# First stage of a DiT trunk on one Trainium2 core: 24 instead of 32 modulation halves on TensorE, row norms and gates taken earlier, background pieces begun later

## The chip, the cores and the metric

The kernel runs on one core of a Trainium2 chip. The metric is the device time of one execution in microseconds, as a median of several runs. All times of single instructions below come from one profiled execution of the kernel before.

## The reference

Batch 1, 256 rows of x and 256 rows of ctx, width 2048, two layers, everything in float32. Cut to what matters here:

```
def reference(x, c, ctx, c_ctx, w_ada, ...):
    for layer in range(2):
        # six modulation vectors a layer, for x and for ctx
        mx = split(silu(c) @ w_ada[layer] + b_ada[layer], 6)
        mc = split(silu(c_ctx) @ w_ada[layer] + b_ada[layer], 6)
        h_x = rms_norm(x, g_pre_mix[layer]) * (1 + mx[1]) + mx[0]
        if layer == 0:                       # ctx feeds layer 0 alone
            h_c = rms_norm(ctx, g_pre_mix[0]) * (1 + mc[1]) + mc[0]
            y_x = attention_deltanet_mixer(h_x, h_c, w_in, ...) @ w_out
        else:
            y_x = fourier_mix(h_x) @ w_fourier
        x = x + mx[2] * rms_norm(y_x, g_post_mix[layer])
        f_x = swiglu(rms_norm(x, ...) * (1 + mx[4]) + mx[3], w_gate, w_up, w_down)
        x = x + mx[5] * rms_norm(f_x, g_post_ffn[layer])
    return x

def deltanet_inputs(qkv_raw, a_raw, b_raw, w_conv, a_log, dt_bias):
    ...                                      # conv, silu, l2 norms of q, k, v
    beta = sigmoid(b_raw)
    g = -exp(a_log) * softplus(a_raw + dt_bias)   # the gates
```

The weights are read from HBM once, some 600 MB in all, and each projection is done as three matmuls on a weight that is split into a rounded part `whi` and a rest `wlo`.

## The kernel before

The kernel is one program whose work is put into engine queues at build time; every engine then runs its queue in order. The text below is about its first stage, which ends near 195.5 us, and about the background work that follows it.

**First stage.** The first two modulation vectors of layer 0 (for x and for ctx) come from a matrix `ada_s`, cut into 32 pieces (16 column blocks `k` times two vectors `m`) of two halves each, 64 halves of 512 KB. `ada_half` (L341 on) loads one half (L346) into the next tile of a ring of borrowed buffers (`RING0`, `RING`) and computes it on one of two engines, by the letter that `WHO` has for its piece. A half on TensorE ("p") is 8 float32 matmuls with 2 columns (16 entries in the trace), which serve x and ctx at once; after the second half ScalarE copies the two sums into `aacc` (tile names K, L354). A half on VectorE ("d") is two multiply-and-sum instructions `ada_dot` (L274) over 128x1024, one for x with the row vector `cb`, one for ctx with `KTOK` or `VTOK`. `WHO` is 'pd' sixteen times: half of the pieces on each engine.

**Norms and transposes.** For ctx and then for x, ScalarE sums the squares of both row blocks (L389, with a ZT buffer as scratch), `rstd` (L305 on: a square root on ScalarE, the rest on VectorE) gives the reciprocal norms, VectorE scales the identity with them into `dg` (L392), and TensorE multiplies the rows with `dg`, which transposes and normalises at once (`turned`, 32 matmuls of 128 columns each for ctx and for x, each of them two entries in the trace). `PRE` says how many halves are put in between: four at each of four places.

**Projection.** Then a loop over 16 blocks `k` runs, with halves issued up to index 4k+8, `mod_k(k-1)` (VectorE adds the sums of a block into `gz`, L419 to L421, ScalarE and GpSimd make the modulated input `hT`) and `proj_k(k-2)`: 42 float32r matmuls of 256 columns against one 128x928 block of `w_g0`, whose `whi` is made on ScalarE (L197) and whose `wlo` on VectorE (L203). `w_g0` holds the first heads of the delta-net and the 32 columns of its gates (`pab`).

**Gates.** After the loop the gates are computed: transposes of `pab` on TensorE, then `exp_fine` (L449 on; an exponential and a logarithm on ScalarE and four small instructions on VectorE) on 128 columns, one more logarithm (L480), and `exp_fine` again on 16 columns of the constant vector `smallr`, whose result is `ea`; `gg` (L484) needs both. ScalarE must load another function table each time that it changes between silu, exponential and logarithm.

**Background.** The ten later modulation vectors come from `ada_d`, 320 pieces of 512 KB. Each is a DMA into one of the two `araw` buffers and one `ada_dot` on VectorE (L285, L274). During the mixer one piece is put in whenever the builder's count of TensorE time has moved on by `MRATE` = 4.3 us (`every`, L147; `step`, L581). Later stages put in pieces at rates of their own, and `ada_until` puts in at once what a stage needs and hasn't got (among them, at the Fourier layer's output projection, up to nine vectors).

## Time and profile before

| what | us |
|---|---|
| median of 3 runs | 2524.68 |
| lowest and highest | 2523.31, 2525.12 |
| profiled execution, its own time | 2527.05 |
| span of its trace | 2525.2 |
| TensorE busy in the span | 2388.6 (95%) |
| VectorE busy | 1775.6 (70%) |
| ScalarE busy | 1274.6 (50%) |
| GpSimd busy | 332.5 (13%) |

The mean granted clock of TensorE is 0.97 of full speed. An engine's busy share is an average over the whole span; the first stage is some 8% of it. In the views, PE is TensorE, DVE is VectorE, ACT is ScalarE, POOL is GpSimd and SP is the engine that issues the loads.

### The profile page before, as it was taken

The numbers are of one execution on the slowest core, as the hardware profiler recorded it, in microseconds if no ns is written. First come the engines' busy times: TensorE is split into PE (matmuls) and PEld (weight loads), VectorE is DVE, ScalarE is ACT, GpSimd is POOL, SyncE is SP. The second block draws the span as 40 slices with busy tenths as digits, with TensorE's granted clock in tenths as the row PEclk, the third lists the DMA queues.
The fourth block names the chain that finished last, engine by engine and source line by source line (L and its number), as shares of the span: only waits on it lengthen the run. The fifth ranks groups of instructions, "written<-read, shape, count | busy, mean of one in ns | idle before, by whom it ended". The sixth has DMA issues, their size and how long they took to land.

```text
span 2525.2 us, 39613 instructions
## 1 busy us (share of the span) xinstructions
PE 2388.6 (95%) x14520; PEld 2022.8 (80%) x14520; DVE 1775.6 (70%) x3204; ACT 1274.6 (50%) x2298; POOL 332.5 (13%) x286
## 2 busy tenths in 40 slices
PE   7999888978799999999999999899999999999997
PEld 7998678867677788888888887697788888888886
DVE  4678788778657777877778788747666665555556
ACT  3337433544465654554445454646654554445455
POOL 1214434245431100000000000101100000000001
PEclk7999989989899999999999999999999999999998
DMA  6675778677837569999898998636577777666665
GB/s 252 244 288 197 236 224 272 208 245 253 263 130 237 197 228 316 312 312 317 319 318 312 315 322 308 211 102 217 191 235 242 232 237 234 193 191 189 191 201 191
DMA packets 218483, 611.04 MB, mean 242 GB/s; under 512 B 68905, under 2 KB 69913, under 8 KB 217521
## 3 DMA queue, kind: packets, MB, share of 16 engines
q1 hardware_dynamic: 168016, 581.59, 68.7%
q10 hardware_dynamic: 46528, 15.21, 2.6%
q0 software_dynamic: 3744, 11.71, 1.4%
q8 instruction: 114, 1.87, 0.3%
q14 instruction: 81, 0.66, 0.1%
HBM read 595.03 MB, written 13.40 MB: 241 GB/s over the span
## 4 chain that ended last, share of the span: by engine, by line
PE 70%; DVE 10%; DMA 6%; issue 3%; ACT 2%; POOL 1%; SPq 0%; ACTq 0%; DVEq 0%; POOLq 0%
PE acc L132 65%; PE sm L132 4%; DMA araw<-in_ada_d 4%; DVE araw L274 3%; DVE S L1153 1%; PE sm L1236 1%; DVE wlo L203 1%; POOL wlo L203 1%; ACT whi L197 1%; DVE C L513 1%; DVE T L729 0%; DMA T<-dy 0%; DVE T L731 0%; DMA T<-dz 0%; DMA raw<-in_w_dn 0%
## 5 line engine op out<-in xcount | busy, mean ns | idle before, releaser
L197 ACT ACTIVATE whi<-raw 128x512 fp32r<-128x512 f32 (+1 forms) x1306 | 817.9, 630 | 858.4 <-DVE wlo L203 489.1
L203 DVE TENSOR_TENSOR wlo<-raw,whi 128x512 fp32r<-128x512 f32 x1140 | 788.7, 699 | 469.8 <-ACT whi L197 468.1
L132 PE MATMUL acc<-whi,S 128*128 128x512 f32 x3312 | 1047.1, 394 | 8.1 <-ACT whi L197 3.7
L132 PEld LDWEIGHTS acc<-whi,S 128*128 128x128 f32 x3312 | 626.7, 190 | 139.5 <-ACT whi L197 4.5
L132 PE MATMUL acc<-wlo,S 128*128 128x512 f32 x1656 | 651.0, 393 | 3.8 <-DVE wlo L203 1.9
L274 DVE SCALAR_TENSOR_TENSOR araw<-araw,cb 128x1024 f32<-128x1024 f32 x320 | 415.6, 1300 | 66.9 <-DMA araw<-in_ada_d 66.3
L132 PEld LDWEIGHTS acc<-wlo,S 128*128 128x128 f32 x1656 | 314.1, 190 | 69.0 <-POOL wlo L203 2.9
L203 POOL TENSOR_TENSOR wlo<-raw,whi 128x512 fp32r<-128x512 f32 x166 | 245.7, 1493 | 445.2 <-ACT whi L197 429.3
L132 PE MATMUL acc<-S,whi 128*128 128x256 f32 x1152 | 235.1, 296 | 5.1 <-ACT whi L197 3.4
L132 PEld LDWEIGHTS acc<-S,whi 128*128 128x128 f32 x1152 | 193.3, 201 | 5.8 <-ACT whi L197 3.6
L132 PE MATMUL acc<-S,wlo 128*128 128x256 f32 x576 | 169.7, 296 | 2.0 <-POOL wlo L203 2.0
L1113 POOL DMA_DIRECT2D drow<-K x4 | 2.0, 508 | 1273.9 <-DVE K L1111 1273.9
L132 PE MATMUL acc<-whi,ZT 128*128 128x512 f32 x384 | 122.1, 392 | 0.0
L132 PEld LDWEIGHTS acc<-S,wlo 128*128 128x128 f32 x576 | 115.9, 201 | 3.5 <-POOL wlo L203 2.6
L132 PE MATMUL acc<-whi,KCH 128*128 128x512 f32 x320 | 110.7, 402 | 1.1 <-ACT whi L197 1.1
L132 PE MATMUL acc<-whi,A 128*128 128x512 f32 x312 | 106.0, 395 | 0.0
L132 PE MATMUL acc<-whi,T 128*128 128x512 f32 x296 | 99.5, 392 | 0.0
L132 PEld LDWEIGHTS acc<-whi,ZT 128*128 128x128 f32 x384 | 72.1, 188 | 15.3
L132 PE MATMUL acc<-wlo,KCH 128*128 128x512 f32 x192 | 78.0, 406 | 4.3 <-DVE wlo L203 4.1
L132 PE MATMUL acc<-wlo,ZT 128*128 128x512 f32 x192 | 75.6, 394 | 0.2 <-POOL wlo L203 0.2
L132 PEld LDWEIGHTS acc<-whi,KCH 128*128 128x128 f32 x320 | 62.2, 195 | 15.2 <-ACT whi L197 1.5
L132 PE MATMUL acc<-wlo,T 128*128 128x512 f32 x176 | 68.8, 391 | 0.0
(437 smaller groups left out, 2829.2 us busy)
## 6 DMA issues: line engine op xcount, KB each, us to landing
raw<-in_w_gu SPq DMA_DIRECT2D x347, 512.0 KB, 4.4
araw<-in_ada_d SPq DMA_DIRECT2D x320, 512.0 KB, 4.8
raw<-in_w_dn SPq DMA_DIRECT2D x179, 512.0 KB, 4.4
raw<-in_w_att SPq DMA_DIRECT2D x40, 512.0 KB, 4.4
raw<-in_w_gdn SPq DMA_DIRECT2D x34, 512.0 KB, 4.8
raw<-in_w_out SPq DMA_DIRECT2D x30, 512.0 KB, 3.7
ZT<-in_ada_s SPq DMA_DIRECT2D x24, 512.0 KB, 3.7
raw<-in_w_four SPq DMA_DIRECT2D x21, 512.0 KB, 3.7
```

The lines of the kernel that those rows point to most:

```text
L132: nc.tensor.matmul(out, l, r, start=start, stop=stop)
L197: S.activation(hi[:, :w], raw[:, c:c + w], AF.Copy)
L203: eng.tensor_sub(lo[:, :w], raw[:, c:c + w], hi[:, :w].bitcast(F32))
L274: V.scalar_tensor_tensor(out=junk, in0=w, scalar=1.0, in1=rows, op0=ALU.mult, op1=ALU.mult, accum_out=dst)
L513: V.scalar_tensor_tensor(out=ca[:, :, lo:hi], in0=pv[:, :, lo + o:hi + o], scalar=wconv[:, blk, j:j + 1], in1=ca[:, :, lo:hi], op0=ALU.mul ...
L1113: nc.gpsimd.dma_start(drow.rearrange("h k p -> (h k) p"), gt)
L1153: V.scalar_tensor_tensor(out=x[:, t, sl], in0=y[:, t, sl], scalar=r, in1=x[:, t, sl], op0=ALU.mult, op1=ALU.add)
L1236: nc.tensor.transpose(p[:, i * P:(i + 1) * P], hv[t][:, i * P:(i + 1) * P], ident)
```

## The change

It does six things.

1. `WHO` becomes 'pd' four times and then 'pdd' eight times: 12 pieces on TensorE instead of 16 (24 halves and not 32), 20 on VectorE instead of 16 (40 halves and not 32).
2. `PRE` becomes (2, 6, 4, 4).
3. All four sums of squares are put in first, one `rstd` works on four columns, and four scalings of the identity follow; before, ctx's norms were done ahead of x's squares.
4. `exp_fine` moves up, and `ea` is computed at the very start.
5. In `proj_k` the gates' 32 columns come first and not next to last.
6. After `every(MRATE)` the due time of the first background piece is moved on by `QUIET` = 24 us of counted TensorE time.

```
-WHO = 'pd' * 16
-PRE = (4, 4, 4, 4)
+WHO = 'pd' * 4 + 'pdd' * 8
+PRE = (2, 6, 4, 4)
 LEAD = 8
+QUIET = 24.0
...
+    ea = C([P, 16], "ea")
+    V.tensor_copy(ea, exp_fine(smallr[:, 1, :], [P, 16]))
...
     for i, (src, name) in enumerate(srcs):
         for t in range(2):
             S.activation(zt([P, D], BF16), src[:, t], AF.Square, accum_out=ssq[:, 2 * i + t:2 * i + t + 1])
-        r0 = rstd(ssq[:, 2 * i:2 * i + 2], 2, D)
+    r0 = rstd(ssq, 4, D)
+    for i in range(2):
         for t in range(2):
-            V.tensor_scalar_mul(dg[:, i, t], ident, r0[:, t:t + 1])
+            V.tensor_scalar_mul(dg[:, i, t], ident, r0[:, 2 * i + t:2 * i + t + 1])
+    for i, (src, name) in enumerate(srcs):
         halves(PRE[2 * i])
...
     def proj_k(k):
         w = wk.pop(k)
+        mm3w(pab[0:32], w[1], slice(2 * P, 2 * P + 32), k, k == 0, k == KC - 1)
         for b in range(4):
...
-        mm3w(pab[0:32], w[1], slice(2 * P, 2 * P + 32), k, k == 0, k == KC - 1)
         mm3w(p1, w[1], slice(2 * P + 32, 3 * P + 32), k, k == 0, k == KC - 1)
...
-    ea = exp_fine(smallr[:, 1, :], [P, 16])
...
     every(MRATE)
+    pace[1] += QUIET
```

`exp_fine` itself is the same at its new place, and its lines, like all that stand below a new line, have other numbers in the changed kernel: L274 is L275 there, L457 is L338, L459 is L340, L480 is L486, L516 is L521, L419 to L421 are L441 to L443, L203 is L204.

**VectorE at the very start, before.** `col` holds the norms, `C` is `dg`, the tiles `araw_213` and `KCH_217` are halves:

```order
L308 TENSOR_SCALAR col_180<-col_169 128x2
L310 RECIPROCAL col_179<-col_179 128x2
L312 TENSOR_TENSOR col_184<-col_179 128x2
L313 TENSOR_TENSOR col_184<-col_184,col_180 128x2
L314 TENSOR_SCALAR col_184<-col_184 128x2
L315 TENSOR_TENSOR col_179<-col_179,col_184 128x2
L392 TENSOR_SCALAR C_26_170<-ident,col_179 128x128 x2
L375 COPY T_17_161<-sm_221 128x2x256
L274 SCALAR_TENSOR_TENSOR E_16_160,K_15_157<-araw_213,cb 128x1024
```

The same place in the changed kernel (`K_17_167` is `aacc`):

```order
L309 TENSOR_SCALAR col_194<-col_179 128x4
L275 SCALAR_TENSOR_TENSOR E_18_170,K_17_167<-araw_253,cb 128x1024
L311 RECIPROCAL col_193<-col_193 128x4
L275 SCALAR_TENSOR_TENSOR E_18_170,K_17_167<-araw_253,KTOK_107 128x1024
L313 TENSOR_TENSOR col_198<-col_193 128x4
L275 SCALAR_TENSOR_TENSOR E_18_170,K_17_167<-KCH_257,cb 128x1024
L314 TENSOR_TENSOR col_198<-col_198,col_194 128x4
L275 SCALAR_TENSOR_TENSOR E_18_170,K_17_167<-KCH_257,VTOK_108 128x1024
L315 TENSOR_SCALAR col_198<-col_198 128x4
L441 TENSOR_REDUCE gz<-K_17_167 128x4
L316 TENSOR_TENSOR col_193<-col_193,col_198 128x4
L413 TENSOR_SCALAR C_28_180<-ident,col_193 128x128 x4
```

The norms now stand between the four dots of the first two VectorE halves, and `dg` comes behind those and behind the first block's sum. (Two small instructions on `gz`, L442 and, behind `dg`, L443, aren't shown; the first stands between the last two rows.)

**VectorE in a step of the projection loop, before.** `wlo` of one `w_g0` block in two parts, the dots of two halves, one sum:

```order
L203 TENSOR_TENSOR wlo_1061<-raw_1058,whi_1060 128x512
L274 SCALAR_TENSOR_TENSOR E_16_160,K_15_157<-araw_1002,VTOK_108 128x1024
L203 TENSOR_TENSOR wlo_1065<-raw_1058,whi_1064 128x416
L419 TENSOR_REDUCE gz<-K_15_157 128x4
L420 TENSOR_TENSOR gz<-gz,bada 128x4
L421 TENSOR_SCALAR gz<-gz,gains 128x2
L274 SCALAR_TENSOR_TENSOR E_16_160,K_15_157<-ZT_1090,cb 128x1024
L274 SCALAR_TENSOR_TENSOR E_16_160,K_15_157<-ZT_1090,KTOK_107 128x1024
L274 SCALAR_TENSOR_TENSOR E_16_160,K_15_157<-ZT_1094,cb 128x1024
```

A step at about the same place in the changed kernel, from one `wlo` to the next:

```order
L204 TENSOR_TENSOR wlo_1033<-raw_1030,whi_1032 128x512
L275 SCALAR_TENSOR_TENSOR E_18_170,K_17_167<-araw_974,cb 128x1024
L204 TENSOR_TENSOR wlo_1037<-raw_1030,whi_1036 128x416
L275 SCALAR_TENSOR_TENSOR E_18_170,K_17_167<-araw_974,VTOK_108 128x1024
L441 TENSOR_REDUCE gz<-K_17_167 128x4
L275 SCALAR_TENSOR_TENSOR E_18_170,K_17_167<-ZT_1062,cb 128x1024
L442 TENSOR_TENSOR gz<-gz,bada 128x4
L275 SCALAR_TENSOR_TENSOR E_18_170,K_17_167<-ZT_1062,KTOK_107 128x1024
L443 TENSOR_SCALAR gz<-gz,gains 128x2
L275 SCALAR_TENSOR_TENSOR E_18_170,K_17_167<-ZT_1066,cb 128x1024
```

Where every step had four dots, three steps together now have sixteen, and dots stand between the small instructions that make a block's sum.

**ScalarE behind the first stage, before.** KCH and ZT are outputs of the convolution (silu), the K tiles belong to the gates, `whi_1981` is the third load after the projection loop:

```order
L516 ACT_TABLE_LOAD
L516 ACTIVATE ZT_1854<-C_268_1896 128x512
L480 ACT_TABLE_LOAD
L480 ACTIVATE K_243_1798<-K_243_1798 128x128
L457 ACT_TABLE_LOAD
L457 ACTIVATE K_245_1808<-smallr 128x16
L509 ACTIVATE C_269_1903<-acc_430,wconv 128x512
L459 ACT_TABLE_LOAD
L459 ACTIVATE K_246_1809<-K_246_1809 128x16
L509 ACTIVATE C_270_1910<-sm_431,wconv 128x256
L197 ACTIVATE whi_1981<-raw_1979 128x512
```

The same place in the changed kernel (`whi_1913` is the same load):

```order
L521 ACT_TABLE_LOAD
L521 ACTIVATE KCH_1786<-C_260_1825 128x512
L340 ACT_TABLE_LOAD
L340 ACTIVATE K_239_1743<-K_239_1743 128x128
L514 ACTIVATE C_262_1839<-acc_430,wconv 128x512
L521 ACT_TABLE_LOAD
L521 ACTIVATE ZT_1790<-C_261_1832 128x512
L514 ACTIVATE C_263_1846<-sm_431,wconv 128x256
L198 ACTIVATE whi_1913<-raw_1911 128x512
L486 ACT_TABLE_LOAD
```

Between the last load's `whi` and this one stood eight table loads; now there are five. The two of `ea` are gone from here, and the one of the logarithm (L480, now L486) comes behind the load.

## Rows read from the trace of the kernel before

**Rows 1.** The page's section 4: the chain that ended last, by line.

```profile
PE acc L132 65%; PE sm L132 4%; DMA araw<-in_ada_d 4%; DVE araw L274 3%; DVE S L1153 1%; PE sm L1236 1%; DVE wlo L203 1%; POOL wlo L203 1%; ACT whi L197 1%; DVE C L513 1%; DVE T L729 0%; DMA T<-dy 0%; DVE T L731 0%; DMA T<-dz 0%; DMA raw<-in_w_dn 0%
```

**Rows 2.** Windows of four stretches: busy time of each engine, granted clock, DMA share.

```profile
core 0: us, PE busy (x) PEld busy (x) DVE busy (x) ACT busy (x) POOL busy (x), PEclk, DMA share, GB/s
120.00:140.00 20.00, 20.00 (x175) 19.66 (x173) 16.49 (x33) 5.67 (x14) 3.03 (x5) 1.00 0.89 317
...
200.00:220.00 20.00, 15.59 (x116) 15.19 (x115) 14.85 (x34) 14.90 (x22) 5.29 (x5) 0.91 0.56 188
...
660.00:680.00 20.00, 14.38 (x318) 10.46 (x316) 13.81 (x30) 8.57 (x19) 8.60 (x8) 1.00 0.78 270
...
1760.00:1770.00 10.00, 8.29 (x48) 6.47 (x49) 9.92 (x22) 8.16 (x21) 2.60 (x2) 1.00 0.78 254
```

**Rows 3.** Timeline of TensorE in 18 to 70 us, from the first half on.

```profile
start us, us, engine line op out<-in xcount [idle before <-releaser]
20.33 3.54 PE L132 MATMUL sm<-c2c,OG 128*128 128x2 f32 x16 [6.03 <-DMA OG<-in_ada_s]
23.74 2.05 PE L132 MATMUL sm<-C,S 128*128 128x128 f32 x8
...
46.93 3.57 PE L132 MATMUL sm<-c2c,ZT 128*128 128x2 f32 x16 [4.18 <-DMA ZT<-in_ada_s]
...
68.27 0.37 PE L132 MATMUL acc<-S,whi 128*128 128x256 f32 x1
```

**Rows 4.** Waits of the load queue (SP), 0 to 190 us: total us, times, longest.

```profile
SPq L346 <- ACT ZT L389: 20.8, 2, 19.4
```

**Rows 5.** Timeline of VectorE: one step of the projection loop, and the last dot's end.

```profile
128.15 1.20 DVE L203 TENSOR_TENSOR wlo<-raw,whi 128x512 fp32r<-128x512 f32 x1 [1.58 <-ACT whi L197]
...
132.69 1.23 DVE L274 SCALAR_TENSOR_TENSOR E<-ZT,KTOK 128x1024 bf16<-128x1024 f32 x1
...
133.96 1.23 DVE L274 SCALAR_TENSOR_TENSOR E<-ZT,cb 128x1024 bf16<-128x1024 f32 x1
...
136.78 1.20 DVE L203 TENSOR_TENSOR wlo<-raw,whi 128x512 fp32r<-128x512 f32 x1 [1.58 <-ACT whi L197]
...
182.20 0.07 DVE L274 DVE_READ_ACCUMULATOR E<-ZT,VTOK 128x1 f32 x1
```

**Rows 6.** Groups of VectorE in 68.3 to 195.6 us: busy, mean ns | idle before.

```profile
L203 DVE TENSOR_TENSOR wlo<-raw,whi 128x416 fp32r<-128x416 f32 (+1 forms) x31 | 25.7, 835 | 26.9 <-ACT whi L197 26.8
```

**Rows 7.** Timeline of TensorE: one half, and the last matmuls of two projection steps.

```profile
129.86 1.85 PE L132 MATMUL sm<-c2c,raw 128*128 128x2 f32 x16
...
190.48 0.29 PE L132 MATMUL sm<-S,whi 128*128 128x256 f32 x1
...
195.50 0.28 PE L132 MATMUL sm<-S,whi 128*128 128x256 f32 x1
```

**Rows 8.** Timeline of ScalarE behind the first stage, 195 to 212 us.

```profile
197.36 1.28 ACT L516 ACT_TABLE_LOAD   x1 [0.92 <-DVE C L513]
198.66 0.63 ACT L516 ACTIVATE KCH<-C 128x512 f32<-128x512 f32 x1
...
211.94 2.18 ACT L197 ACTIVATE whi<-raw 128x512 fp32r<-128x512 f32 x4
```

**Rows 9.** Timeline of TensorE behind the first stage, 212 to 216 us.

```profile
212.62 0.38 PE L132 MATMUL acc<-S,whi 128*128 128x256 f32 x1 [3.44 <-ACT whi L197]
213.97 0.38 PE L132 MATMUL acc<-S,wlo 128*128 128x256 f32 x1 [0.97 <-POOL wlo L203]
...
215.41 0.63 PE L132 MATMUL acc<-S,whi 128*128 128x256 f32 x2
```

**Rows 10.** The chain that ended last, in 640 to 720 us: start, us, what.

```profile
664.33 5.49 DMA araw<-in_ada_d
669.85 2.72 DVE araw L274 x2
...
698.88 6.55 DMA araw<-in_ada_d
```

More of the change, by code (lines that the diff above doesn't have):

```diff
@@ L327, in rstd_m2, with exp_fine @@
         return r
+    def exp_fine(x, shape):
+        n = int(np.prod(shape[1:]))
+        names = "a b c"[:2 * len(shape) - 3]
+        pat = "p (" + names + ") -> p " + names
+        dims = {c: v for c, v in zip("abc", shape[1:])}
+        v = lambda t: t[:, 0:n].rearrange(pat, **dims) if len(shape) > 2 else t[:, 0:n]
+        y, l = v(T([P, 256], "K1", 3)), v(T([P, 256], "K1", 3))
+        S.activation(y, x, AF.Exp)
+        V.tensor_scalar_max(l, y, 1e-30)
+        S.activation(l, l, AF.Ln)
+        V.tensor_tensor(out=l, in0=x, in1=l, op=ALU.subtract)
+        V.tensor_scalar(l, l, -1e-3, 1e-3, ALU.max, ALU.min)
+        V.scalar_tensor_tensor(out=y, in0=l, scalar=1.0, in1=y, op0=ALU.add, op1=ALU.mult)
+        return y
+    ea = C([P, 16], "ea")
+    V.tensor_copy(ea, exp_fine(smallr[:, 1, :], [P, 16]))
     aacc = T([P, KC, 2, 2, 2], "K1", 3)
@@ L447, in trunk @@
             wk[k - SK_P + 1] = load_w(a["w_g0"][k - SK_P + 1], 928)
-    def exp_fine(x, shape):
-        n = int(np.prod(shape[1:]))
-        names = "a b c"[:2 * len(shape) - 3]
-        pat = "p (" + names + ") -> p " + names
-        dims = {c: v for c, v in zip("abc", shape[1:])}
-        v = lambda t: t[:, 0:n].rearrange(pat, **dims) if len(shape) > 2 else t[:, 0:n]
-        y, l = v(T([P, 256], "K1", 3)), v(T([P, 256], "K1", 3))
-        S.activation(y, x, AF.Exp)
-        V.tensor_scalar_max(l, y, 1e-30)
-        S.activation(l, l, AF.Ln)
-        V.tensor_tensor(out=l, in0=x, in1=l, op=ALU.subtract)
-        V.tensor_scalar(l, l, -1e-3, 1e-3, ALU.max, ALU.min)
-        V.scalar_tensor_tensor(out=y, in0=l, scalar=1.0, in1=y, op0=ALU.add, op1=ALU.mult)
-        return y
     abT = e2([32, 512])
```

## The prediction

> **What bounds the kernel now.** I read the chain that ended last first: over the whole program 65% of it is TensorE in the projections (acc, L132), 4% are TensorE's small tiles, among them the halves and the transposes, and some 7% are background pieces, their loads and their dots [rows 1]. So TensorE is the bound in general, and the background is where it isn't. The windows say where. In the steady first stage TensorE is full, 20.00 of 20 us at a granted clock of 1.00, beside VectorE at 16.49; behind that stage TensorE has 15.59 of 20, at the mixer's end 14.38 of 20, in the Fourier output projection 8.29 of 10 with VectorE at 9.92 [rows 2]. TensorE's timeline shows how the stage begins: the first half comes at 20.33 after a wait for its load, ctx's transposes from 23.74, a wait of 4.18 us before 46.93, and the projection from 68.27 [rows 3]; its last matmul starts at 195.50 [rows 7]. The load queue's waits name a cause for part of the slow start: it stood 19.4 us behind a ZT buffer that the squares of x (L389) were to free [rows 4].
>
> **Start of the first stage: 0 us (-5 to +4).** The squares of x go early, so the 19.4 us of the load queue and the 4.18 us of TensorE behind it go. What is late next is `dg`. It needs the square root, which on ScalarE stands behind the evacuation of halves 0 and 1. These are the only TensorE work that is left before the transposes: from 20.33, at 3.54 us each, until 27.4 [rows 3]. Table load, 1.28 as behind the stage [rows 8], and square root end near 29.1. On VectorE the small instructions of the norm then alternate with dots of 1.27 us (132.69 to 133.96 [rows 5]), of which three come behind the square root: 3.8 us, plus about 1.3 for the rest, so `dg` is there near 34.2. Ctx's transposes start at 34.2 and not at 23.74; TensorE stands for 6.8 us. Then 64 transposes and six halves are left. Before, 60 transposes and the same six halves took from about 29 (20.33, two halves and the first 2.05 us of transposes) to 68.27, with the wait of 4.18 and partly at the lower clock. With 13 us at the lower clock behind the idle time and the rest at the full one I get 66, with a second stretch at the lower clock 72: about 69, between 63 and 72, against 68.27. Moving `ea` costs two table loads in a time when ScalarE has nothing to do: 0.
>
> **Steady part: +4 us (-8 to +14).** TensorE loses 8 halves at 1.85 us [rows 7], 14.8 us; that is what could come back at most if VectorE kept up. VectorE gets 8 halves, 16 dots at 1.27: +20.2 us. It idled 26.8 us in this stretch waiting for `whi` [rows 6], so in sum it has room, but not where it's needed. A step takes 8.63 us before (128.15 to 136.78) with 1.58 idle, so 7.05 of work [rows 5]: four dots are 5.07, the rest, `wlo` and sums, 2.0 to 2.1. Three steps now hold 16 dots and not 12: 20.2 + 3 x 2.1 = 26.6 us, 8.9 a step, while TensorE has 5.02 for the projection (190.48 to 195.50 [rows 7]) and 2/3 of a pair of halves (3.7), 7.5. VectorE becomes the bound and a step is 0.25 us longer, not shorter. The first five steps hardly use VectorE's room, since the dots are let in only eight halves ahead of the step. From the sum of block 5, some 22 us behind the start of the projection, VectorE still has 54 dots (68.3), ten `wlo` pairs (16) and nine sums (5), with bits 91 us; then three projection steps remain, as before, where the last dot ended at 182.20 and the stage at 195.8 (13.6 us, 14.5 now). Sum: 69 + 22 + 91 + 14.5 = 196.5, against 195.8: +0.7 (with the start). That holds if VectorE never waits. If it waited 1.58 us in each of ten steps as before, it would be +16; but those waits were for ScalarE's `whi`, whose buffers TensorE freed late, and TensorE is early now. On the other side, if the tail is one step shorter than I count, and the five first steps use half a step of room each, it is -8. Nearest to the rows is a quarter of the waits: +4.
>
> **Gates and what follows the stage: -5 us (-7 to -2).** Between 197.36 and 211.94 ScalarE is in a row of table loads, 1.28 us each (197.36 to 198.66), and TensorE has run dry: it waits 3.44 us for `whi` and 0.97 for `wlo`, and then runs matmuls of 0.63 us for two, at the lower clock, against 0.40 (half of that lost for some four us: 1 to 2) [rows 8, 9]. Three table loads and some 0.8 us of small activations no longer stand ahead of that `whi`: 3 x 1.28 + 0.8 = 4.6 us earlier, so the 3.44 goes, most of the 0.97, and the clock needn't fall. Three background dots no longer stand between VectorE's gate instructions. Taken: 3.44 + 0.3 + 1.3 = 5.0. Cover: should the load of that block be late, the first term stays. The gates' columns first bring 5.02/42 x 6, less than 0.7, and only to the transposes: 0.3.
>
> The page's rows show a load of 1.28 us and the next activation 0.02 us behind its end [rows 8]. The Trainium skill, ScalarE: Activation LUTs, section What ACT_TABLE_LOAD costs, puts a drain of 1.38 us on top, 2.66 a switch; by that the three loads would be worth 8.0 us. The rows don't show that drain.
>
> **Background in the mixer: -4 us (-8 to 0).** 24 us at 4.3 us a piece are six pieces fewer by the end of the mixer. There TensorE is not full (14.38 of 20 [rows 2]), and the chain runs through the pieces: 5.49 us of a load and 2.72 of two dots at 664, 6.55 of a load at 698.88 [rows 10]. Six dots are 7.6 us of VectorE; two such waits would go or move by some us. Upper bound 8, the dots and no more; lower 0, since other loads stand in the same queue and the next wait (a projection block by the same 16 DMA engines) ends nearly as late. I take half: 4.
>
> **Fourier output projection: +2 us (0 to +6).** Of the six pieces four come back inside that projection, where nine vectors must be there. VectorE is at 9.92 of 10 [rows 2], so four dots, 5.1 us, may stand on the path; they are put in where TensorE was still full, which hides some. Two come back in the last feed-forward, where VectorE is half idle: 0.
>
> **Sum.** 0 + 4 - 5 - 0.3 - 4 + 2 = -3.3 us on the profiled execution of 2527.05. That one is 2.37 above the median of 2524.68 (its span is 2525.2). On the median: 2521.4, a change of 0.13%; about 0.2%, 5.0 us, is what a measurement can tell from no change.
>
> **Rivals.**
>
> (a) Faster: VectorE's room is used. The 26.8 us of idle are more than the 20.2 added; if the steps float freely, VectorE ends at 182.2 - 26.8 + 20.2 = 175.6 and the stage with it at 189. Then the steady term is -6.5 and not +4, and the time 2511. For it: the ring lets loads run ahead and the stalled queue [rows 4] is gone. Against: the dots stand in VectorE's queue between `wlo` pairs, which wait for TensorE.
>
> (b) Slower: TensorE, which now waits in each step, loses its clock. Waits of 4.18 and 3.44 us were followed by halves of 3.57 us and matmuls of 0.63 for two, the 1.2 GHz level [rows 3, 9]. If the 1.4 us a step gather into such waits every third step (a step with two halves takes TensorE 8.7, one with none 5.0, so 3.9 us are left there), five steps run at half clock, 5 us more each; what VectorE's bound doesn't cover of that, some 3 us each, adds 15: 2536. [...] Against it: at the mixer's end TensorE waits for 28% of the time at a granted clock of 1.00 [rows 2]. The Trainium skill says the same as (b): TensorE: Matmul & The Clock Gate, section HAM oscillation — how this bites in real kernels, describes a loop whose waits for data throttle TensorE again at every tile. The rows bear that out at two long waits and speak against it at short ones.
>
> (c) The later background brings nothing: the six pieces are on the chain only because something has to be. Then the mixer term is 0, the Fourier term +4, and the time 2527.5: still no change that can be measured.
>
> **How the numbers follow.** The forecast, 2521.4, and (c) together 0.40, of which the forecast 0.29 and (c) 0.11; (a) 0.36 in two parts, 0.27 with its time near 2511 and 0.09 in which the mixer gives 8 as well, 2507; (b) 0.18; 0.06 for a start at 72 with the low clock kept in the loop, 2531. (a) is faster by over 0.2%; of the 0.40, a twentieth is too, 0.02. Faster 0.38, same 0.38, slower 0.24. The range 2508 to 2536 leaves out the lower part of (a) and the upper part of (b).
>
> **What would show it.** The projection's first matmul near 69 us; a step of 8.9 us, VectorE full from 100 to 180 us and TensorE waiting for `hT` or `wlo`; the stage's end near 199; no wait of 3.44 us for `whi` behind it and a granted clock of 1.00 there; the chain at 660 to 710 without two loads of `ada_d`; VectorE at 10 of 10 near 1760. Wrong would be: a stage that ends before 192 (then (a)), or windows in 90 to 190 with a granted clock under 0.9 (then (b)).

## The result, and the profile after

The changed kernel takes 2545.17 us (median of 4 runs, 2543.09 to 2551.92), beside it the kernel before 2523.99: a ratio of 1.0091, interval 1.0068 to 1.0114. A second series on one chip gave 1.0096 (1.0066 to 1.0126). The forecast was 2521.4 with a range to 2536: the change is slower by 0.9%, and outside the range.

The page of the changed kernel, busy times and the chain by line:

```profile
PE 2390.8 (94%) x14392; PEld 2012.8 (79%) x14392; DVE 1791.7 (70%) x3231; ACT 1278.9 (50%) x2297; POOL 349.9 (14%) x286
...
PE acc L133 64%; PE sm L133 7%; DMA araw<-in_ada_d 4%; DVE araw L275 2%; POOL wlo L204 2%; DVE C L518 1%; DVE wlo L204 1%; DMA T<-dy 1%; DVE E L275 1%; DVE S L1159 1%; PE sm L1242 1%; ACT whi L198 1%; DMA OG<-in_ada_s 1%; DMA T<-dz 0%; DVE K L713 0%
```

TensorE has 128 matmul records fewer than before (eight halves of 16) and is busy 2 us longer: what was left ran more slowly (the windows below show it for the first stage, pad64 for the feed-forwards). "PE sm" went from 4% of the chain [rows 1] to 7%, and VectorE's first-stage dots ("DVE E") are on it now. The windows of the first stage show where:

```profile
core 0: us, PE busy (x) PEld busy (x) DVE busy (x) ACT busy (x) POOL busy (x), PEclk, DMA share, GB/s
100.00:120.00 20.00, 17.99 (x112) 17.74 (x112) 16.79 (x34) 2.85 (x7) 3.17 (x2) 0.67 0.63 226
120.00:140.00 20.00, 17.32 (x106) 16.89 (x105) 16.63 (x31) 5.28 (x13) 6.19 (x4) 0.67 0.56 202
140.00:160.00 20.00, 17.93 (x122) 17.33 (x122) 14.68 (x27) 8.13 (x20) 7.02 (x6) 0.76 0.65 243
160.00:180.00 20.00, 19.39 (x139) 19.05 (x138) 19.83 (x38) 2.85 (x7) 2.80 (x3) 0.80 0.75 284
180.00:200.00 20.00, 15.71 (x109) 15.10 (x109) 16.20 (x29) 6.47 (x15) 7.19 (x5) 0.83 0.58 204
```

Where before had 20.00 of 20 us and a granted clock of 1.00 [rows 2], TensorE now stands still for 2 to 4 us of most 20, and its clock is at 0.67 to 0.83 until 200. But for one row, where VectorE has 19.83, neither engine is full. The projection itself had not begun later. TensorE's timeline of the changed kernel:

```profile
33.34 6.13 PE L133 MATMUL sm<-C,S 128*128 128x128 f32 x32 [6.36 <-issue]
...
68.75 0.36 PE L133 MATMUL sm<-S,whi 128*32 128x256 f32 x1
...
102.01 0.58 PE L133 MATMUL acc<-S,wlo 128*128 128x256 f32 x1 [3.09 <-DVE wlo L204]
...
104.10 3.41 PE L133 MATMUL sm<-c2c,araw 128*128 128x2 f32 x16
```

The first transposes are at 33.3 (34.2 was worked out, against 23.74 in [rows 3]), TensorE stood 6.4 us for them, and the projection runs from 68.75, against 68.27 (its first four matmuls stand at 57.85, between halves). Then comes a pattern of three steps. At 102.01 TensorE has waited 3.09 us for `wlo`; what follows runs at half speed, the half at 104.10 in 3.41 us where [rows 7] has 1.85. VectorE at the same time:

```profile
101.27 0.69 DVE L204 TENSOR_TENSOR wlo<-raw,whi 128x512 fp32r<-128x512 f32 x1
...
123.09 0.16 DVE L441 TENSOR_REDUCE gz<-K 128x4 f32<-128x8 f32 x1 [6.23 <-ACT K L374]
...
129.35 1.64 DVE L275 SCALAR_TENSOR_TENSOR E<-ZT,VTOK 128x1024 bf16<-128x1024 f32 x1
131.02 1.62 DVE L275 SCALAR_TENSOR_TENSOR E<-ZT,cb 128x1024 bf16<-128x1024 f32 x1
132.69 1.23 DVE L275 SCALAR_TENSOR_TENSOR E<-ZT,KTOK 128x1024 bf16<-128x1024 f32 x1
```

The `wlo` that TensorE waited for at 102.01 was made at 101.27, behind six dots. Then VectorE in turn waits 6.23 us for the sums of a pair of halves on TensorE (K). Each engine waits for the other once in three steps, and three steps take 29 to 32 us (from 91.19 to 123.62, 155.41 and 184.54 for the same `wlo`) against 25.9 before (three times 8.63 [rows 5]). VectorE is busy for 25.9 to 26.3 us of each of these three stretches, close to the 26.6 that were worked out; what comes on top is its waiting. Three or four of the dots of a group take some 1.63 us and not 1.22. GpSimd makes `hT` beside them (125.38 to 131.57 for the row at 129.35), but it does so too at 113.67 to 116.84, where two dots take 1.23 and 1.21 us.

To see what every stretch contributes, the table takes six points that each trace has once (in brackets: the same in the first trace of before, which is longer in the mixer): the first read of the gates' transposes, `lbmg` (the gates' end), the first output of the last attention projection (mixer's end), the last `VTOK` of the Fourier mix, the last norm behind the Fourier output projection, and VectorE's last instruction, each by its start. Stretches in us, from the timelines:

| stretch | before, second trace (first) | after | difference |
|---|---|---|---|
| start to gates' read | 196.4 (196.3) | 212.1 | +15.7 |
| to `lbmg` | 23.8 (23.9) | 18.4 | -5.4 |
| mixer | 501.5 (507.9) | 502.6 | +1.1 |
| output projection, feed-forward, Fourier mix | 942.7 (943.9) | 949.0 | +6.3 |
| Fourier output projection | 103.6 (103.3) | 110.4 | +6.8 |
| last feed-forward | 750.0 (749.9) | 752.7 | +2.8 |
| together | | | +27.3 |

So 16 us come from the first stage, and three stretches further down, two of which contain no line of the change, add 15.9, about three times what the gates give.

### The profile page after: what moved, and what is told of

Read it like the earlier page. It is cut to its first block, busy times and chain, and to the rows that moved or that the text cites. A ratio compares the mean times of both kernels' runs of the same rounds, so it can differ in the third digit from the quotient of the medians.

```text
span 2545.2 us, 39392 instructions
## 1 busy us (share of the span) xinstructions
PE 2390.8 (94%) x14392; PEld 2012.8 (79%) x14392; DVE 1791.7 (70%) x3231; ACT 1278.9 (50%) x2297; POOL 349.9 (14%) x286
## 3 DMA queue, kind: packets, MB, share of 16 engines
q8 instruction: 113, 1.85, 0.3%
## 4 chain that ended last, share of the span: by engine, by line
PE 72%; DVE 11%; DMA 7%; issue 5%; ACT 3%; POOL 2%; SPq 0%; ACTq 0%; DVEq 0%; POOLq 0%
PE acc L133 64%; PE sm L133 7%; DMA araw<-in_ada_d 4%; DVE araw L275 2%; POOL wlo L204 2%; DVE C L518 1%; DVE wlo L204 1%; DMA T<-dy 1%; DVE E L275 1%; DVE S L1159 1%; PE sm L1242 1%; ACT whi L198 1%; DMA OG<-in_ada_s 1%; DMA T<-dz 0%; DVE K L713 0%
## 5 line engine op out<-in xcount | busy, mean ns | idle before, releaser
L204 DVE TENSOR_TENSOR wlo<-raw,whi 128x512 fp32r<-128x512 f32 x1140 | 782.0, 693 | 452.6 <-ACT whi L198 451.1
L275 DVE SCALAR_TENSOR_TENSOR araw<-araw,cb 128x1024 f32<-128x1024 f32 x320 | 414.2, 1295 | 67.0 <-DMA araw<-in_ada_d 66.7
L204 POOL TENSOR_TENSOR wlo<-raw,whi 128x512 fp32r<-128x512 f32 x166 | 246.3, 1496 | 423.9 <-ACT whi L198 406.6
```

Of the source, the lines that this page charges most:

```text
L204: eng.tensor_sub(lo[:, :w], raw[:, c:c + w], hi[:, :w].bitcast(F32))
L275: V.scalar_tensor_tensor(out=junk, in0=w, scalar=1.0, in1=rows, op0=ALU.mult, op1=ALU.mult, accum_out=dst)
```

## The experiments

Ratios are to the kernel before on the same chip, with the 95% interval.

**The change again (after_again).** No edit. 

> The changed kernel again, unaltered, beside the kernel before on one chip. In the two profiles at hand the changed kernel's first stage ends 16 us later, and besides its matmuls in the feed-forwards follow each other at 0.2284 us where before's did at 0.2267 (0.7%), which makes some 9 of the 21 us. Theory A: the cadence belongs to the chip or the hour, not to the change; then on one chip both have the same cadence and the change costs about 12 us (ratio 1.005). Rival B: the cadence comes with the change (its later pieces lie otherwise beside the matmuls); then the ratio is 1.0085 again and the cadence 0.7% longer.

1.0096 (1.0066 to 1.0126), and the longer cadence of the feed-forwards is there again (179.34 us, see pad64 below), while who_alone, on the same chip, has the short one: rival B. The chip is not the reason.

**The dealing put back (who_back).**

```
-WHO = 'pd' * 4 + 'pdd' * 8
+WHO = 'pd' * 16
```

> The changed kernel with the halves dealt out as before (32 on TensorE). Theory A: the dealing costs the 16 us of the first stage, because VectorE becomes the bound and TensorE, which waits for it, drops to its lower clock; then this is 16 us faster than the changed kernel, its stage ends near 195 with a granted clock of 1.00 from 100 us on, and it keeps the 5.5 us behind the stage: 4 us or so faster than before. Rival B: the new start (norms behind the dots, first transposes at 33 us) costs as much; then it is within 5 us of the changed kernel.

1.0061 (1.0042 to 1.0081): 9 us faster than the changed kernel, not 16. Its runs lie between 2527 and 2541 us; in the profiled one, the slowest, the gates' read is at 209.3. Its windows, columns as above:

```profile
104.00:112.00 8.00, 7.99 (x54) 7.70 (x52) 6.91 (x13) 1.05 (x3) 0.69 (x1) 0.74 0.43 150
112.00:120.00 8.00, 8.00 (x49) 7.91 (x48) 4.72 (x10) 2.84 (x7) 1.43 (x2) 0.62 0.61 239
120.00:128.00 8.00, 7.99 (x71) 7.75 (x70) 4.42 (x6) 2.24 (x6) 1.44 (x2) 1.00 0.54 165
```

TensorE is full here (7.99 and 8.00 of 8) and its clock falls all the same, to 0.62. So waits are one way to lose the clock and not the only one. Both theories had this wrong.

**The dealing alone (who_alone).** The kernel before with the same line the other way round. 

> The kernel before with only the new dealing (24 halves on TensorE, 40 on VectorE). Theory A: it alone makes the first stage 15 to 18 us longer, with a granted clock of 0.65 to 0.85 in 100 to 200 us: 15 to 18 us slower than before. Rival B: the dealing is harmless where the norms come first for ctx (TensorE then begins 10 us earlier) and only the two together starve TensorE: within 5 us of before.

1.0075 (1.0047 to 1.0104); the gates' read is at 212.3, 15.9 us later than in before, and the clock in 100 to 200 us is 0.73 to 0.83. Theory A: the dealing by itself makes the whole loss of the first stage. The cadence in its feed-forwards is before's.

**The background from its old time (quiet0).**

```
-QUIET = 24.0
+QUIET = 0.0
```

> The changed kernel without the later begin of the background. Theory A: the later begin gives 6 us at the mixer's end and takes 7 us in the Fourier output projection, where four pieces come back: within 3 us of the changed kernel, with +6 at the mixer's end and -7 behind the Fourier layer. Rival B: the pieces at the mixer's end are hidden and the 6 us there came from elsewhere; then this is 7 us faster than the changed kernel.

1.0113 (1.0084 to 1.0142), the same as the changed kernel within the intervals. The Fourier output projection is back at 103.6 us from 110.4, the mixer takes 504.2 against 502.6. The first half of theory A is seen in the trace (the 7 us), its second half, 6 us at the mixer's end, does not stand out of the spread of the whole mixer (see quiet_alone for the mixer's last part).

**64 unused bytes (pad64).** In the kernel before:

```
+    pad = C([P, 16], "pad")
+    nc.gpsimd.memset(pad, 0.0)
     aacc = T([P, KC, 2, 2, 2], "K1", 3)
```

> The kernel before with one unused tile of 64 bytes a partition, set once at the start by GpSimd, allocated ahead of the borrowed buffers, so that every tile behind it (whi, wlo, raw, ZT and so on) lies 64 bytes further on, as in the changed kernel, where ea stands there. Nothing else is changed. So far the two kernels without an early ea have 0.2267 us from matmul to matmul in the feed-forwards, the three with it 0.2284. Theory A: the address does it; then the feed-forwards here have 0.2284 and the kernel is 9 us slower than before. Rival B: the cadence comes from something else in the change; then 0.2267 and no difference to before.

1.0040 (1.0026 to 1.0055): 10 us slower, from a tile that nobody reads. ScalarE's evacuations of the gate projection in the first feed-forward, of which each pair stands for the same number of matmuls, show the cadence. First and fifth pair, in the second trace of before, in pad64, and in the changed kernel:

```profile
1292.43 1.28 ACT L1257 ACTIVATE E<-acc 128x512 f32<-128x512 f32 x2
...
1470.11 1.28 ACT L1257 ACTIVATE E<-acc 128x512 f32<-128x512 f32 x2
```

```profile
1292.00 1.28 ACT L1259 ACTIVATE E<-acc 128x512 f32<-128x512 f32 x2
...
1471.34 1.28 ACT L1259 ACTIVATE E<-acc 128x512 f32<-128x512 f32 x2
```

```profile
1306.58 1.28 ACT L1263 ACTIVATE E<-acc 128x512 f32<-128x512 f32 x2
...
1485.91 1.28 ACT L1263 ACTIVATE E<-acc 128x512 f32<-128x512 f32 x2
```

177.68, 179.34 and 179.33 us for the same work, with TensorE full in all three. In all the eighteen traces of this study it is one of these two numbers (177.7 or 179.3), and it is the longer one exactly where the borrowed buffers lie 64 bytes further on. Theory A. The early `ea`, 64 bytes a partition, is allocated ahead of those buffers; in the kernel before it was a piece of one of them.

**Only the gates' columns first (gates_first).** `pab`'s line moved up in `proj_k`, in the kernel before. 

> The kernel before with only the gates' 32 columns first in a projection step. With the dealing put back, the changed kernel still lost TensorE's full clock at 106 to 118, 138 to 148 and 168 to 176 us, though TensorE never stood still there. Theory A: the six matmuls of 32 columns now stand against a half's matmuls of 2 columns, and the clock falls behind such a stretch of thin work; then here too the granted clock is below 0.95 in several windows of 100 to 180 us and the stage ends 8 to 14 us later than before. Rival B: the fall comes from the new start (the norms, PRE); then the stage is as before within 2 us, clock 1.00 from 100 us on.

1.0006 (0.9994 to 1.0019), clock 1.00 from 92 us on, gates' read at 195.3: theory A falls, the thin matmuls of the gates beside a half don't lower the clock by themselves.

**Only the squares first, with PRE (squares_pre).**

```
-PRE = (4, 4, 4, 4)
+PRE = (2, 6, 4, 4)
...
-        r0 = rstd(ssq[:, 2 * i:2 * i + 2], 2, D)
...
+    r0 = rstd(ssq, 4, D)
+    for i in range(2):
```

> The kernel before with only the four squares first, one rstd, and PRE (2, 6, 4, 4). By theory A of gates_first the projection begins within 3 us of before, the granted clock is 1.00 from 100 us on and the stage ends within 3 us of before. By rival B the clock falls in 100 to 180 us here and not in gates_first: the stage ends 8 to 14 us later.

0.9984 (0.9971 to 0.9997): a small gain, only just clear of noise, the gates' read 3.6 us earlier than in before (192.8), clock 1.00 from 92 us to the gates' read. Rival B of gates_first falls as well. So the new start is the one part of the change that pays in the first stage. With the early `ea` beside it the start is not so early: the first transposes come at 27.37 us here and at 33.34 in the changed kernel. The square root of the norms (L309, L310), on ScalarE, in squares_pre and in the changed kernel:

```profile
21.09 1.28 ACT L309 ACT_TABLE_LOAD   x1
22.39 0.20 ACT L309 ACTIVATE col<-col 128x4 f32<-128x4 f32 x1
```

```profile
27.09 0.17 ACT L374 ACTIVATE K<-sm 128x2 f32<-128x2 f32 x1 [3.02 <-PE sm L133]
27.27 1.28 ACT L310 ACT_TABLE_LOAD   x1
28.57 0.20 ACT L310 ACTIVATE col<-col 128x4 f32<-128x4 f32 x1
```

Here it stands right behind the squares. In the changed kernel ScalarE does `ea`'s instructions between the squares, with two table loads, and the root has its place behind the evacuation of the first halves (L374), for which it waits 3.02 us; on VectorE the norm's instructions alternate with dots. In the two other pairs that differ in the early `ea` and its bytes alone it is the same: best has the first transposes at 33.95 and combo_ea at 34.11, squares_pre and combo (below) at 27.37 and 27.30. So the early `ea` costs what the early squares had gained.

**The dealing and the gates' place put back (who_gates_back).** 

> The changed kernel with the dealing and the place of the gates' columns both as before; kept are the squares first, PRE, the early ea and the later background. Theory A: no fall of the clock in 100 to 180 us, the stage ends at 195 or so, 5 us are won behind it, 6 at the mixer's end, 7 go in the Fourier projection and 9 by the cadence: about 5 us slower than before in all, mean clock 0.973 as in before. Rival B: the clock still falls as with the dealing alone put back, and the time is that kernel's, 15 us slower than before.

1.0047 (1.0031 to 1.0062), 10 us slower (2528.7 against 2518.8), twice the 5 us that theory A had; clock 1.00 from 92 us on, gates' read at 194.8. Theory A as far as the stage goes. Between this and who_back stands only the place of the gates' columns, and that place does nothing in the kernel before. Why the two together lose the clock in who_back, and not in all of its runs, stays open.

**TensorE given the work back, VectorE not relieved (both_engines).** In the changed kernel, for the four pieces without a TensorE piece in their step:

```
+        if i // 2 in (12, 18, 24, 30):
+            x = sm()
+            for kk in range(8):
+                mm(x[:, 0:2], raw[:, kk * P:(kk + 1) * P], c2c[:, h * 8 + kk, :], kk == 0, kk == 7)
         ada_dot(raw, cb[:, h], aacc[:, k, m, 0, h:h + 1], junk)
```

> The changed kernel, in which the four pieces that have no TensorE piece beside them in their step (12, 18, 24, 30: eight halves) are computed on TensorE as well, into a tile that nobody reads. TensorE's work in the stage is that of the kernel before again, VectorE's that of the changed one; nothing of the result changes. Theory A, the clock: TensorE's waits behind VectorE drop its clock, and the dropped clock is most of the 16 us; with the eight halves in the gaps the clock stays up and the stage ends at 195 to 205 us, no later than the changed kernel's 211. Theory B, VectorE: its dots alone set the end, so it is about 211 again. Theory C, handing over: TensorE's work lies in series with VectorE's; then eight more halves make it later, 215 to 226.

1.0117 (1.0091 to 1.0143); the gates' read is at 223.0, 11 us later than in the changed kernel. The time lies in theory C's range, and A falls: filling TensorE's gaps doesn't hold the clock. C's reason is not shown with that. Columns as above:

```profile
160.00:180.00 20.00, 20.00 (x120) 19.78 (x120) 15.60 (x26) 1.98 (x7) 3.53 (x3) 0.65 0.42 156
```

TensorE is full in this window, at 0.65. In the whole stage it stands still for only 4.3 us (the table below), so what makes it late here is its clock.

**VectorE relieved, TensorE not loaded (moved_left_out).** The same four pieces without dots:

```
+        if i // 2 in (12, 18, 24, 30):
+            V.tensor_copy(aacc[:, k, m, :, h], raw[:, 0:2])
+            return
```

> The changed kernel, in which the same four pieces (eight halves) are loaded but not multiplied at all: a copy of two columns stands in for their dots, so that part of the first two modulation vectors is left out of the computation. VectorE's load is that of the kernel before, TensorE's that of the changed one. Theories B and C: without the sixteen dots the stage ends at 180 to 192, earlier than before's 195, since TensorE has 14.8 us less to do. Theory A: TensorE still waits somewhere in each group of steps and its clock still falls; then the stage ends at 195 to 205.

1.0037 (1.0015 to 1.0059); gates' read at 198.8, 13 us earlier than in the changed kernel and 2.4 later than before. What it waited for, TensorE and VectorE in 68 to 222 us (total us, times, longest):

```profile
PE acc L133 <- ACT whi L198: 6.5, 4, 2.1
...
PE acc L133 <- DVE wlo L204: 1.2, 1, 1.2
```

```profile
DVE wlo L204 <- ACT whi L198: 18.2, 10, 4.0
DVE gz L444 <- ACT K L374: 11.6, 4, 4.7
```

This is theory A's range: TensorE was spared 14.8 us, VectorE's idle time is that of before (34.7 us from 70 us to the gates' read, 32.6 in before), and yet the stage is no shorter. The waits are a part of the reason, the clock is the larger one, as the table below shows.

**What the first stage's time is made of.** From 70 us to the gates' read, columns as above, in this order: before, the changed kernel, who_back, both_engines, moved_left_out:

```profile
70.00:196.28 126.28, 126.21 (x1055) 124.34 (x1053) 93.71 (x175) 44.18 (x104) 28.18 (x32) 0.97 0.72 259
70.00:212.07 142.07, 128.18 (x924) 124.74 (x924) 113.33 (x206) 44.60 (x104) 44.93 (x36) 0.82 0.68 250
70.00:209.29 139.29, 138.32 (x1055) 135.26 (x1053) 93.52 (x175) 46.59 (x109) 31.20 (x36) 0.87 0.68 251
70.00:223.02 153.02, 148.75 (x1045) 146.66 (x1043) 113.46 (x202) 42.70 (x99) 41.75 (x32) 0.78 0.62 228
70.00:198.82 128.82, 120.73 (x919) 117.93 (x918) 94.09 (x177) 43.14 (x100) 37.52 (x34) 0.86 0.74 268
```

An estimate from these rows splits each length into TensorE's standstill, the part of its busy time that the lower clock took (busy time times 1 - clock), and the rest, its work as it would be at the full clock:

| us | length | standstill | taken by the lower clock | work at the full clock |
|---|---|---|---|---|
| before | 126.3 | 0.1 | 4 | 122 |
| changed kernel | 142.1 | 13.9 | 23 | 105 |
| who_back | 139.3 | 1.0 | 18 | 120 |
| both_engines | 153.0 | 4.3 | 33 | 116 |
| moved_left_out | 128.8 | 8.1 | 17 | 104 |

So the new dealing spares TensorE some 17 us of work, and loses 14 by standing still and 19 by the clock. In moved_left_out the clock takes 13 us more than in before and standstill 8, together more than the 18 that TensorE was spared; in who_back and both_engines nearly everything that is lost is lost by the clock. That the dealing alone brings the 16 us about is shown by who_alone, and who_back shows that the clock can fall without it; why it falls is not shown.

**The changed kernel with 192 unused bytes (after_pad).**

```
     ea = C([P, 16], "ea")
+    pad = C([P, 48], "pad")
+    nc.gpsimd.memset(pad, 0.0)
```

> The changed kernel with an unused tile of 192 bytes a partition beside ea, so that all tiles behind it lie 256 bytes and not 64 further on than in the kernel before. If the place of the tiles costs 10 us in the feed-forwards, as the 64 unused bytes did in the kernel before, and if 256 bytes are as good as none, this is 10 us faster than the changed kernel (ratio to before 1.0055 and not 1.0096) with 0.2267 us from matmul to matmul. If every shift costs, it is as the changed kernel.

1.0062 (1.0042 to 1.0082), and the cadence is before's, 177.70 us from the first pair to the fifth:

```profile
1308.24 1.28 ACT L1265 ACTIVATE E<-acc 128x512 f32<-128x512 f32 x2
...
1485.94 1.28 ACT L1265 ACTIVATE E<-acc 128x512 f32<-128x512 f32 x2
```

A shift by 256 bytes costs nothing, one by 64 does. Other shifts were not tried.

**What is left of the change (best).** Squares first, PRE, early `ea` with the 192 bytes. 

> What the runs so far leave of the change: the squares first, PRE and the early ea, with the 192 unused bytes; dealing, the gates' place and the begin of the background as before. Squares and PRE alone measured 0.9984 of before. If the early ea is worth its 5 us behind the stage, this is at 0.996 to 0.998, some 5 to 10 us faster than before; if the mixer swallows them, at 0.998 to 1.000.

0.9993 (0.9981 to 1.0005): no change that can be measured, though `lbmg` is 4.3 us earlier than in before. The mixer, 505.6 us in this trace, swallowed it.

**The later background alone (quiet_alone), and the kernel before again (before_copy).**

```
     every(MRATE)
+    pace[1] += 24.0
```

> The kernel before with only the later begin of the background (24 us of counted TensorE time). The prediction had -4 us (-8 to 0) at the mixer's end and +2 (0 to +6) in the Fourier output projection. Theory A, from the two traces: four pieces come back ahead of the Fourier weights and cost 7 to 8 us there, while the mixer gives nothing that stands out of its own spread of some 10 us; then this is 3 to 8 us slower than before (1.001 to 1.003), with +7 between the Fourier mix and the last feed-forward. Rival B: the mixer's end does give 6 us, and the two cancel: 0.999 to 1.001, with -6 at the mixer's end in the trace.

> The kernel before, unaltered, for a second trace. The first one's execution took 2527.05 us, 6 to 8 above the median of the executions since. Theory: the mixer's length varies by some 10 us from execution to execution (its background loads fall differently beside its own), the other stages by 1 or 2; then the first stage ends within 2 us of the first trace's, the mixer's end lies 3 to 12 us earlier, and the feed-forwards have 0.2267 us from matmul to matmul. Rival: the difference is spread evenly over the program, as of a slower chip.

before_copy: 1.0002 (0.9990 to 1.0013), its stage, feed-forwards and Fourier layer within 2 us of the first trace, its mixer 6.5 us shorter: the theory. quiet_alone: 0.9999 (0.9987 to 1.0010); the Fourier output projection takes 109.9 us and not 103.6, and the mixer 490.3. Gain and loss cancel: rival B. The length of the whole mixer varies too much to show the gain: in the traces without the later begin it is 494.5 to 507.9 us (eight traces, mean 502.0), with it 490.3 to 506.9 (ten, mean 499.8). The mixer's last part shows it. From VectorE's last `C<-acc,rope` to the mixer's end, in before_copy and in quiet_alone:

```profile
650.05 0.68 DVE L940 TENSOR_TENSOR C<-acc,rope 128x512 f32<-128x512 f32 x1
...
721.64 1.09 ACT L983 ACTIVATE C<-acc 128x512 f32<-128x512 f32 x2
```

```profile
646.72 0.68 DVE L940 TENSOR_TENSOR C<-acc,rope 128x512 f32<-128x512 f32 x1
...
711.51 1.09 ACT L983 ACTIVATE C<-acc 128x512 f32<-128x512 f32 x2
```

That is 71.6 us against 64.8. In all eight traces without the later begin this part takes 70.5 to 75.2 us (mean 73.5), in the ten with it 64.8 to 71.1 (mean 68.4). So the later begin gives some 5 us at the mixer's end and loses 6.3 in the Fourier output projection, and the medians show no difference. The loss is plain. The chain of the changed kernel in the Fourier output projection:

```profile
1741.94 4.50 DMA araw<-in_ada_d
...
1746.52 1.25 DVE araw L275 x2
...
1747.79 4.28 DMA araw<-in_w_four
```

TensorE behind it:

```profile
1752.77 1.52 PE L133 MATMUL acc<-ZT,T 128*128 128x512 f32 x2 [3.70 <-ACT ZT L198]
```

The pieces that are caught up hold the two `araw` buffers, in which the next weight block is to come: it is asked for at 1747.79, when the last dot is done, lands 4.28 us later, and TensorE waits 3.70 us for what ScalarE makes of it. quiet_alone has the same wait (3.92 us); before_copy, quiet0 and combo have none over 1.2 us in this stretch.

**A version that keeps what paid (combo, combo_ea).** The kernel before with squares_pre, the later begin, and

```
-F0RATE = 3.9
+F0RATE = 3.7
```

so that the first feed-forward, where VectorE has room, catches the pieces up. 

> The kernel before with the squares first, PRE (2, 6, 4, 4) and the later begin of the background, and with one more number: in the first feed-forward a background piece comes every 3.7 and not 3.9 us of counted TensorE time, so that 293 pieces (before 290, with the later begin alone 284) are in the queue ahead of the Fourier weights and none has to be caught up there. If the 6.6 us that the later begin alone costs in the Fourier projection come from the pieces that are caught up, they are gone here, the 10 us at the mixer's end and the 3 of the start stay: 0.994 to 0.997 of before. If the feed-forward has no room for ten more pieces, 0.998 to 1.000.

> The same with the early ea and its 192 unused bytes. If the 5 us behind the first stage reach the end, 2 to 5 us faster than combo; if the mixer swallows them, as it did in the run without the later background, the same as combo within 2 us.

combo: 0.9962 (0.9946 to 0.9978), 2510.12 us against 2518.84: faster than both kernels. Its Fourier output projection takes 103.8 us, so the 6.3 us that quiet_alone lost there came from the pieces that were caught up there, and the feed-forward has the room. F0RATE was not changed alone. combo_ea: 0.9978 (0.9962 to 0.9993), not faster than combo: the early `ea` isn't worth its place.

## Why the prediction was wrong, point by point

**Start, 0 us.** Right: the first transposes, which need `dg`, came at 33.3, the projection ran from 68.75. squares_pre shows what the prediction missed, that the part without `ea` gains 3 us; the cost of 0 for moving `ea` was wrong by that, as its instructions stand ahead of the norm's root on ScalarE.

**Steady part, +4 (-8 to +14).** This is the step that failed: +15.7 by the trace, and who_alone gives 15.9 for the dealing alone. VectorE's work was worked out rightly (26.6 us for three steps; 25.9 to 26.3 measured), but the stage doesn't run at the larger of two sums of work: three steps took 29 to 32 us. The prediction added a quarter of VectorE's old waits, all for `whi`, since "TensorE is early now". It put at nothing the wait that came: VectorE stands for the sums of a pair of halves on TensorE (`gz<-K`), 14.8 us in four waits between 68 and 212 (none over 0.5 us in before), beside 7.5 us for `whi`. With the pairs in two steps of three TensorE is early in one step and late in the next. And it counted TensorE's 7.5 us a step at the full clock, where the granted clock was 0.67 to 0.83. The dots of 1.63 us (17 of the 64 behind 70 us, some 7 us in all) are within what VectorE's sum had allowed.

What stood in the text as rival (b), with a chance of 0.18, is nearest to what happened: TensorE's waits of 3.09, 1.90, 2.08 and 3.51 us, one to each three steps, windows under 0.9, and the 1.2 GHz level. Its price, 15 on top of the steady +4, makes 19 against the 15.7 measured; its time, 2536, still fell short, for want of what lies behind the stage. Its picture was not complete: both_engines and who_back lose the clock with TensorE full, and so does the changed kernel itself, which has TensorE at 6.00 of 6 us from 114 to 120 us and a clock of 0.51 right behind that:

```profile
114.00:120.00 6.00, 6.00 (x56) 5.97 (x54) 2.86 (x6) 0.00 (x0) 2.83 (x2) 1.00 0.71 240
120.00:127.00 7.00, 6.22 (x31) 5.88 (x31) 3.80 (x8) 4.11 (x11) 1.62 (x2) 0.51 0.68 241
```

The Trainium skill's rule that the prediction set beside it (TensorE: Matmul & The Clock Gate, section HAM oscillation — how this bites in real kernels), that waits in a loop throttle TensorE anew each time, agrees with the trace in part: the half behind the wait of 3.09 us at 102.01 took 3.41 us and not 1.85, but the fall at 120 has no such wait ahead of it.

**Gates, -5 (-7 to -2).** Right where it was read, lost further on: 5.4 us from the gates' read to `lbmg`, and in all ten traces with the early `ea` this stretch is 17.4 to 19.9 us against 23.8 to 24.5 in the eight without. TensorE's wait of 3.44 us for `whi` [rows 9] is gone, and the granted clock behind the stage is 1.00 (212 to 232 us) where it was 0.91 [rows 2]. ScalarE's rows of the changed kernel:

```profile
220.86 1.28 ACT L521 ACT_TABLE_LOAD   x1
222.16 0.64 ACT L521 ACTIVATE ZT<-C 128x512 f32<-128x512 f32 x1
222.70 0.46 ACT L514 ACTIVATE C<-sm,wconv 128x256 f32<-128x256 f32 x1
223.05 0.62 ACT L198 ACTIVATE whi<-raw 128x512 fp32r<-128x512 f32 x1
```

The `whi` stands right behind the convolution now. But best and combo_ea show that these 5 us don't reach the end. Most is gone within the first 100 us: from the gates' read to VectorE's first `T<-T` behind `lbmg` it is 93.9 us in the mean of the ten traces with the early `ea` and 95.4 in that of the eight others, 1.4 us apart, and their ranges overlap (87.1 to 97.1 and 93.9 to 96.6). The prediction let every gain ahead of the mixer count in full.

**Mixer, -4 (-8 to 0).** Right in size: some 5 us at the mixer's end, as the last part of the mixer shows over all traces (68.4 against 73.5 us, quiet_alone). The whole mixer of this pair of traces, +1.1, hides it: the trace on which the prediction rested was one of a long mixer (507.9 us; the second 501.5), so the chain's two waits for `ada_d` there [rows 10] were in part that execution's.

**Fourier output projection, +2 (0 to +6).** Too small, and outside its range: 6.8. The prediction priced four dots, 5.1 us. What costs is the buffers: the pieces take the two `araw` tiles that the next weights need, and a load of 4.28 us comes behind them. The prediction had no term for that.

**What no step had, +9.** The early `ea` moves every tile behind it by 64 bytes, and with that a stretch of the feed-forward takes 0.9% longer (pad64's median is 10 us longer). The diff showed the new tile, and no row of before could show its price; the 0 for moving `ea` left it out.

By sum: 15.7 - 5.4 + 1.1 + 6.8, with 9.1 for the feed-forwards and what lies between (6.3 and 2.8), gives 27.3 in the traces; 21 to 24 in the medians. Against the prediction's sum of -3.3 the first stage is 12 more, the addresses 9, the Fourier projection 5, and the whole mixer, by its spread in these two traces, another 5. The stated range, up to 2536, allowed for (b) but for nothing behind the stage, so the dealing's 16 us and the addresses' 9 together took the time out of it.

## What to carry to other kernels

Two engines that hand each other work in a ring don't run at the larger of their two loads: before moving work to the idler one, look where each waits for the other's result, and at the clock that the busier one may lose; the larger of two sums of work is a lower bound. (A dealing of 24 halves in which each step is like the next was not tried here.) Work that is put off has to be fitted in somewhere: here the same delay lost 6.3 us where the pieces took the buffers of the next weights, and none where a full TensorE hid them. And a new constant, however small, should not move the tiles behind it: to see whether it did, compare a long stage that the change doesn't touch.

## What the runs showed of the hardware

- **The place of tiles in SBUF.** With all borrowed buffers 64 bytes further on, a stretch of the feed-forward in which TensorE is full takes 179.34 us and not 177.68; 256 bytes further on it takes 177.70. Nothing else in the rows tells it: the matmuls' idle time is 0 in both. How other distances behave is open.
- **The clock with TensorE full.** Windows of 8 us with 7.99 and 8.00 us of matmuls had granted clocks of 0.74 and 0.62 (who_back), one of 20 with 20.00 had 0.65 (both_engines). Halves, matmuls of two columns, stand in all of them, but they do so too in before, at 20.00 of 20 and 1.00 [rows 2]. Runs of one kernel differ: who_back's mean granted clock is 0.964 to 0.973. What decides it stays open.
- **The mixer's spread.** The same program's mixer took 507.9 and 501.5 us in two executions, while its other stretches agreed within 2 us.
